# A decoder layer on one core: input tiles of the matmuls at two fixed offsets of SBUF, sample state multiplied in halves

## The chip, the cores and the metric

One Trainium2 chip, one of its cores. The metric is the time of one execution on the device in microseconds (us), as the median of the runs of a kernel.

## The reference

One step of a hybrid decoder layer in float32, for 256 prompt tokens and 8 sample tokens (264 columns in all), model width 2048:

```python
def decoder_layer(h, p, conv_buf, xbc_buf, h0, ...):
    h = h + 0.5 * rmsnorm(swiglu(rmsnorm(h, n1), w1_gate, w1_up, w1_down), n1_post)
    mix, cb, xb, hs = token_mixer(rmsnorm(h, n_mix), conv_buf, xbc_buf, h0, w_in, ..., w_out)
    h = h + rmsnorm(mix, n_mix_post)
    h = h + 0.5 * rmsnorm(swiglu(rmsnorm(h, n2), w2_gate, w2_up, w2_down), n2_post)
    gate = sigmoid(rmsnorm(h, n_ple) @ w_ple_gate)
    h = h + rmsnorm(gate * (p @ w_ple_proj), n_ple_post)
    return h, cb, xb, hs
```

The token mixer projects to 81 column tiles of 128, runs a gated convolution of width 31 on 1024 of the channels and a chunked state-space scan (48 heads, 8 groups, state 128) on the rest, and projects back. For each sample token it also reads the old state (`hst`), takes its product with that token's C vector, and writes the new state. The last three rows of the projection's xBC part are an output as well (`xo`).

## The kernel before

All activations lie feature-major: a tile is 128 features by 264 tokens. Every product with a weight matrix is made of three matmuls per 128 x 128 block (`mm3`, lines 242 to 246): weights and inputs are each split into a high half rounded to float32r and the low half that rounding left, and the sum takes high x high (L244), high weights x low input (L245) and low weights x high input (L246). For each of the three the weights are loaded anew and 264 columns of the input stream through.

**Inputs.** `split` (L248) makes an input tile out of a 128 x 264 tile: ScalarE writes the high half, VectorE the low half. `act_tile` (L193) takes the memory for both from a pool, `[P, 2, T]` float32, with 32 buffers of 2112 bytes per partition, the low half 1056 bytes behind the high one. In the built program buffer i begins at byte 89312 + 2112 i of each partition. Since 89312 is 348 x 256 + 224 and 2112 is 8 x 256 + 64, the high halves begin at 224, 32, 96 or 160 modulo 256 in turn, and the low halves 32 further, at 0, 64, 128 or 192. Each of the four kinds carries about a quarter of the matmuls.

**Weights.** They stream in units of up to 16 blocks (`Weights.load`, L135), each unit in halves of 8 blocks: one DMA of 512 KB on SyncE's queue (L150), the rounding on ScalarE (L151), the rest on VectorE (L152). Raw, high and low have four buffers each, and all of these begin at 224 modulo 256. The DMA queue of SyncE carries the weights and all other loads and stores in one order.

**Order.** FFN 1, the first part of the per-layer embedding, the mixer, FFN 2, the rest of the embedding. Most products go through `gemm_one` (L342): one output tile at a time, over 12 to 16 input tiles one after the other. `gemm_first` (L330) begins each product with four output tiles at once, so that one input tile serves four triples, 12 matmuls, in a row. In the mixer, the work of a state-space group (`ssd`, L678; `gate`, L769) is laid among the matmuls by a scheduler that runs when the program is built.

TensorE carries out its matmuls in the program's order, and the trace holds a record of every one of L244 to L246, 18,960 in all. So the n-th record is the n-th matmul of the program, and the input tile that a row of the trace read, and its address, are known from the built program.

**Sample state.** Lines 750 to 754: for each head pair j of a group, 1024 elements per partition of the old state are loaded (8 tokens x 128) into one of two buffers `h0`, GpSimd multiplies them by the C vectors, and VectorE sums each token's 128 products into `ych`.

**xBC rows.** `do_conv` (L598) copies the last 11 columns of each of 40 tiles to `xo`, one tile of 1760 bytes per partition, which L822 stores once at the end.

Of the kernel before, what the change touches and what calls it, by code (L numbers as in the profile page):

```python
# [9 lines left out]
F32 = mybir.dt.float32  # L10
F32R = mybir.dt.float32r
# [8 lines left out]
P = 128  # L20
NP_ = 256
NS = 8
T = NP_ + NS
DM = 2048
# [17 lines left out]
# ---------------------------------------------------------------- layout plan  # L42
def _in_order():
    """Column tiles of the input projection in the order they are computed."""
# [25 lines left out]
def _plan():  # L70
    """Weight units in order of use: (matrix, row tiles, column tiles), row tile slowest."""
# [39 lines left out]
# columns of the small-parameter block  # L111
# [13 lines left out]
class Weights:  # L125
    """Streams the weight units: load, round to float32r, keep what rounding left."""
# [8 lines left out]
    def load(self, between=()):  # L135
        """The next unit, in halves; runs a function of `between` ahead of each half."""
# [29 lines left out]
def kernel(ctx: ExitStack, tc: tile.TileContext, a: dict):  # L166
# [3 lines left out]
    cpool = ctx.enter_context(tc.tile_pool(name="cpool", bufs=1))  # L170
    wpool = ctx.enter_context(tc.tile_pool(name="wpool", bufs=4))
# [5 lines left out]
    # ------------------------------------------------------------ helpers  # L177
# [15 lines left out]
    def act_tile():  # L193
        return apool.tile([P, 2, T], F32R, tag="act", bufs=32, name=nm("act"))

# [32 lines left out]
    def table(name):  # L228
        """Functions that need a table run in program order, so that tables change only here."""
        if order["set"] != name:  # L230
            order["set"] = name
            after(nc.scalar.preload_act_table_set(name).ins)
# [15 lines left out]
    def split(x, gain=None):  # L248
        """float32r halves of x (times a gain per partition)."""
# [9 lines left out]
    class SumSq:  # L259
        """Sum of squares over tiles and partitions, on every partition. The last `direct` tiles  # L260
        go to the tensor engine by themselves."""
# [19 lines left out]
        def add_plain(self, s):  # L281
            """Adds the tile s itself."""
# [16 lines left out]
    def rsqrt(out, x, bias=0.0, scale=1.0):  # L299
        """(scale * x + bias) ** -0.5"""  # L300
        act(out, x, AF.Ln, bias=bias, scale=scale)
        act(out, out, AF.Exp, scale=-0.5)

    def rms_scale(p, n):
        """1 / sqrt(p / n + eps)"""
# [4 lines left out]
    # ------------------------------------------------------------ constants  # L310
# [10 lines left out]
    # ------------------------------------------------------------ residual stream  # L321
# [5 lines left out]
    bg = deque()  # work that fills in between the matrix products  # L327

    # ------------------------------------------------------------ feed-forward
# [22 lines left out]
    def ffn(xs, sq, done):  # L352
        """xs: split gained input; sq: its sum of squares. Calls done(m, y) on each finished
        column tile y (without the input scale); returns eps * (mean square + eps) of the input."""
# [42 lines left out]
    def ffn_scale(p, eq):  # L397
        """1 / 2 / sqrt(mean(y^2) + eps / scale^2): the post-norm of scale * y, halved, where
        eq = eps / scale^2."""
# [13 lines left out]
    # ============================================================ FFN 1  # L413
# [15 lines left out]
    # sample conv history: sums over the saved rows  # L429
# [33 lines left out]
    # y for the post-norm; h . y and y . y (with the gain) for the next pre-norm  # L463
# [22 lines left out]
    # mean square of h + rs y, from the parts  # L486
# [8 lines left out]
    # per-layer embedding projection: independent of the residual stream  # L495
# [13 lines left out]
    # u = rmsnorm(h + rs y), two tiles behind the update of h  # L509
# [15 lines left out]
    # ============================================================ mixer  # L525
# [3 lines left out]
    # causal triangle: row token s, column token l, l >= s  # L529
# [6 lines left out]
    tm = mp.tile([P, 2, 2, NH], F32, name="tm")          # token-major dt, dt*A per chunk  # L536
# [548 lines left out]
```

## Time and profile before

| | |
|---|---|
| median of 3 runs | 2482.04 us |
| lowest and highest | 2472.21 and 2486.53 us |
| span of the profiled execution, first to last instruction | 2479.2 us |
| its own time | not recorded apart from the span, which lies between the lowest and highest run, 2.8 us below the median |
| TensorE | 97% busy |
| VectorE, ScalarE, GpSimd | 64%, 48%, 14% busy |
| DMA | 490 MB, 198 GB/s |
| granted TensorE clock, mean | 0.990 |

A matmul's row in the trace has a start and a duration. The starts are measured; the ends are modelled, and successive matmuls overlap. What a matmul costs in a full stream is therefore the distance from its start to the next one's start, and for a stretch of a stream its length over the number of matmuls in it. The timeline prints starts to 0.01 us.

### The profile page before, as it was taken

The page shows a single profiled execution, that of the slowest core. Times are in us where ns is not written, and L with a number is a line of the kernel's source. Part 1 is how long each engine was busy: PE and PEld are TensorE (multiplying, and loading weights), DVE is VectorE, ACT ScalarE, POOL GpSimd, SP SyncE. Part 2 cuts the span into 40 slices and gives each one's busy share as a digit, 9 for nine tenths or more (in the row PEclk, how much of TensorE's full clock was granted, in tenths as well). Part 3 has the DMA queues.
Part 4 walks back from the last instruction along what each step waited for, and adds up shares of the span by engine and source line. Part 5 has one row for each costly group of instructions (what it writes and reads, how often), then busy time and mean ns, then how long its engine had stood idle before and what let it go on. Part 6 is the DMA issues. An engine that isn't in the chain of part 4 may idle for free.

```text
span 2479.2 us, 47214 instructions
## 1 busy us (share of the span) xinstructions
PE 2405.7 (97%) x19432; PEld 2380.9 (96%) x19432; DVE 1593.6 (64%) x2249; ACT 1179.2 (48%) x1761; POOL 348.6 (14%) x329
## 2 busy tenths in 40 slices
PE   8999999999999999999999999899999999999996
PEld 8999999999999889999998999899999999999996
DVE  6554455545557858979898965855545655555585
ACT  6444444433456465555655454544444443344463
POOL 2500000000015212121112011410000000000142
PEclk9999999999999999999999999999999999999998
DMA  7655555555556665666665547467666776675653
GB/s 242 211 181 180 180 179 179 180 180 181 181 167 214 200 199 191 214 208 197 210 212 187 180 162 231 140 232 235 221 211 221 237 236 206 210 239 191 193 171 114
DMA packets 160201, 489.88 MB, mean 198 GB/s; under 512 B 23360, under 2 KB 40304, under 8 KB 159984
## 3 DMA queue, kind: packets, MB, share of 16 engines
q1 hardware_dynamic: 159984, 486.85, 60.9%
q8 instruction: 152, 2.49, 0.4%
q14 instruction: 65, 0.53, 0.1%
HBM read 465.65 MB, written 22.42 MB: 197 GB/s over the span
## 4 chain that ended last, share of the span: by engine, by line
PE 86%; DVE 7%; DMA 2%; ACT 2%; issue 2%; POOL 1%; SPq 0%; DVEq 0%; ACTq 0%; POOLq 0%
PE acc L244 28%; PE acc L246 28%; PE acc L245 28%; DVE wlo L152 2%; DVE y L213 1%; DVE h L210 1%; DVE tmp L213 1%; ACT whi L151 1%; DVE act L213 1%; PE ps L729 1%; PE ps L296 0%; POOL run L210 0%; DMA ab<-d_cs 0%; PE ps L714 0%; DMA wraw<-in_w 0%
## 5 line engine op out<-in xcount | busy, mean ns | idle before, releaser
L244 PE MATMUL acc<-act,whi 128*128 128x264 f32 x6320 | 1801.0, 288 | 16.8 <-ACT whi L151 8.4
L245 PE MATMUL acc<-act,whi 128*128 128x264 f32 x6320 | 1804.2, 286 | 12.5 <-DVE act L213 6.3
L246 PE MATMUL acc<-act,wlo 128*128 128x264 f32 x6320 | 1802.4, 286 | 3.6 <-DVE wlo L152 3.6
L152 DVE TENSOR_TENSOR wlo<-wraw,whi 128x1024 fp32r<-128x1024 f32 (+1 forms) x806 | 992.3, 1233 | 612.7 <-ACT whi L151 610.0
L151 ACT CAST whi<-wraw 128x1024 fp32r<-128x1024 f32 (+1 forms) x806 | 828.1, 1031 | 994.7 <-PE acc L245 733.5
L245 PEld LDWEIGHTS acc<-act,whi 128*128 128x128 f32 x6320 | 1203.6, 190 | 17.9 <-DVE act L213 8.6
L246 PEld LDWEIGHTS acc<-act,wlo 128*128 128x128 f32 x6320 | 1199.1, 190 | 7.7 <-DVE wlo L152 5.2
L244 PEld LDWEIGHTS acc<-act,whi 128*128 128x128 f32 x6320 | 1186.6, 189 | 19.9 <-ACT whi L151 8.4
L210 POOL TENSOR_TENSOR run<-run,tmp 128x264 f32<-128x264 f32 x135 | 129.8, 962 | 982.3 <-ACT tmp L237 978.8
L210 POOL TENSOR_TENSOR s<-s,eap 128x1024 f32<-128x1024 f32 x24 | 47.3, 1972 | 608.2 <-DMA s<-in_hst 586.4
L213 DVE SCALAR_TENSOR_TENSOR y<-v,vec,y 128x247 f32<-128x247 f32 (+23 forms) x240 | 124.5, 540 | 1.1
L213 DVE SCALAR_TENSOR_TENSOR s<-bb,xds,s 128x128 f32<-128x128 f32 x192 | 52.6, 347 | 62.9 <-POOL s L210 62.9
L210 POOL TENSOR_TENSOR h<-h,cbc 128x1024 f32<-128x1024 f32 x24 | 65.4, 2738 | 165.3 <-DVE y L213 72.1
L210 DVE TENSOR_TENSOR tmp<-acc,rr 128x264 f32<-128x264 f32 x104 | 44.7, 431 | 64.0 <-PE acc L246 63.9
L252 ACT CAST act<-tmp 128x264 fp32r<-128x264 f32 x120 | 48.6, 409 | 62.3 <-DVE tmp L210 47.5
L210 DVE TENSOR_TENSOR tmp<-tmp,acc 128x264 f32<-128x264 f32 x88 | 37.6, 427 | 45.6 <-PE acc L246 44.8
L210 DVE TENSOR_TENSOR act<-tmp,act 128x264 fp32r<-128x264 f32 x120 | 54.3, 457 | 0.0
L210 DVE TENSOR_TENSOR y<-y,acc 128x264 f32<-128x264 f32 x80 | 34.0, 425 | 26.5 <-PE acc L246 26.5
L237 ACT ACTIVATE tmp<-tmp 128x264 f32<-128x264 f32 x112 | 46.8, 418 | 8.3 <-DVE tmp L210 8.0
L237 ACT ACTIVATE tmp<-y 128x264 f32<-128x264 f32 x67 | 28.1, 426 | 42.3 <-DVE y L210 41.2
L213 DVE SCALAR_TENSOR_TENSOR act<-h,vec,act 128x264 fp32r<-128x264 f32 x48 | 35.2, 756 | 6.4 <-ACT act L237 6.4
L237 ACT ACTIVATE act<-h,vec 128x264 fp32r<-128x264 f32 x48 | 23.8, 512 | 31.3 <-POOL h L210 15.2
(148 smaller groups left out, 800.7 us busy)
## 6 DMA issues: line engine op xcount, KB each, us to landing
wraw<-in_w SPq DMA_DIRECT2D x774, 512.0 KB, 4.7
h<-in_hst SPq DMA_DIRECT2D x24, 512.0 KB, 4.9
s<-in_hst SPq DMA_DIRECT2D x24, 512.0 KB, 6.4
out_nss<-s SPq DMA_DIRECT2D x24, 512.0 KB, 2.8
wraw<-in_w SPq DMA_DIRECT2D x32, 256.0 KB, 3.7
ab<-d_cs SPq DMA_DIRECT2D x16, 384.0 KB, 4.2
cbc<-d_bc SPq DMA_DIRECT2D x8, 512.0 KB, 4.2
bb<-d_bc SPq DMA_DIRECT2D x8, 512.0 KB, 7.4
```

The costliest lines, as they stand in the source:

```text
L151: nc.scalar.copy(hi, raw)
L152: nc.vector.tensor_tensor(out=lo, in0=raw, in1=hi.bitcast(F32), op=ALU.subtract)
L210: return (eng or nc.vector).tensor_tensor(out=out, in0=in0, in1=in1, op=op)
L213: return nc.vector.scalar_tensor_tensor(out=out, in0=in0, scalar=scalar, in1=in1, op0=op0, op1=op1)
L237: i = nc.scalar.activation(out=out, in_=in_, func=func, bias=bias, scale=scale)
L244: nc.tensor.matmul(acc, hi, x[:, 0, :], start=first, stop=False)
L245: nc.tensor.matmul(acc, hi, x[:, 1, :], start=False, stop=False)
L246: nc.tensor.matmul(acc, lo, x[:, 0, :], start=False, stop=last)
L252: nc.scalar.copy(t[:, 0, :], x)
L729: nc.tensor.matmul(pd[64 * q : 64 * q + 64, P * c : P * c + P], xdt[c][:, 2 * j + q, :], ab[c][:, 2 * j + q, :], start=True, stop=True,)
```

## The change

The input tiles get a pool of their own, `xpool`, allocated ahead of the weights. A buffer is 576 floats, 2304 bytes, which is 9 x 256, and of these the first 528 are used as before. The pool begins at byte 23264, which is 90 x 256 + 224. So every high half begins at 224 and every low half at 0 modulo 256; the weights stay at 224. The built program has these two offsets for all 18,960 matmuls.

The pool takes 6 KB more per partition. The tile `xo` becomes two rotating tiles of 10 pieces (2 x 440 bytes instead of 1760), each stored by three small DMAs once it is full. The state `h0` is loaded, multiplied and summed in halves of four tokens: 512 elements instead of 1024, three buffers of half the size instead of two.

```diff
+XSTRIDE = 576
...
+    xpool = ctx.enter_context(tc.tile_pool(name="xpool", bufs=32))
     wpool = ctx.enter_context(tc.tile_pool(name="wpool", bufs=4))
...
     def act_tile():
-        return apool.tile([P, 2, T], F32R, tag="act", bufs=32, name=nm("act"))
+        t = xpool.tile([P, XSTRIDE], F32R, tag="act", bufs=32, name=nm("act"))
+        return t[:, : 2 * T].rearrange("p (i t) -> p i t", i=2)
...
-    xo = mp.tile([P, 40, 3 + NS], F32, name="xo")
+    xos = {}
...
+    def xo_piece(i):
+        g = i // 3 if i < 24 else (i - 24) % 8
+        return g // 2, (i - 6 * (g // 2) if i < 24 else 6 + (i - 24) // 8 * 2 + g % 2)
+
+    def xo_runs(q):
+        return [((6 * q, 6), 0), ((24 + 2 * q, 2), 6), ((32 + 2 * q, 2), 8)]
...
     def do_conv(acc, i, out):
-        nc.scalar.copy(xo[:, i, :], acc[:, NP_ - 3 :])
+        q, e = xo_piece(i)
+        if q not in xos:
+            xos[q] = [mp.tile([P, 10, 3 + NS], F32, tag="xo", bufs=2, name=nm("xo")), 0]
+        nc.scalar.copy(xos[q][0][:, e, :], acc[:, NP_ - 3 :])
+        xos[q][1] += 1
+        if xos[q][1] == 10:
+            t = xos[q][0]
+            for (lo, n), src in xo_runs(q):
+                nc.sync.dma_start(a["xo"][:, lo : lo + n, :], t[:, src : src + n, :])
...
         for j in range(3):
-            h0 = mp.tile([P, NS, P], F32, tag="h0", bufs=2, name=nm("h0"))
-            nc.sync.dma_start(h0, a["hst"][3 * g + j])
-            tt(h0, h0, cbc, ALU.mult, nc.gpsimd)
-            nc.vector.tensor_reduce(out=ych[:, j, :], in_=h0, op=ALU.add, axis=AX.X)
+            for b in range(0, NS, 4):
+                h0 = mp.tile([P, 4, P], F32, tag="h0", bufs=3, name=nm("h0"))
+                nc.sync.dma_start(h0, a["hst"][3 * g + j][:, b : b + 4, :])
+                tt(h0, h0, cbc[:, b : b + 4, :], ALU.mult, nc.gpsimd)
+                nc.vector.tensor_reduce(out=ych[:, j, b : b + 4], in_=h0, op=ALU.add, axis=AX.X)
...
-                nc.sync.dma_start(a["xo"], xo)
```

Outside the mixer and the output projection behind it the order of the matmuls is the same row for row. In the mixer the scheduler places the parts of the state-space groups a little differently. On VectorE, in the first group's sample part, the sums of the state stood like this before (`wlo` is the low half of a weight buffer, `ych` the sums, `h` here the product with C):

```order
L152 TENSOR_TENSOR wlo_8_10350<-wraw_8_10348,whi_8_10349 128x1024
L152 TENSOR_TENSOR wlo_0_10405<-wraw_0_10403,whi_0_10404 128x1024
L754 TENSOR_REDUCE ych_9872<-h_496_9873 128x8
L152 TENSOR_TENSOR wlo_8_10411<-wraw_8_10409,whi_8_10410 128x1024
L754 TENSOR_REDUCE ych_9872<-h_497_9877 128x8
L152 TENSOR_TENSOR wlo_0_10479<-wraw_0_10477,whi_0_10478 128x1024
```

and stand like this now:

```order
L153 TENSOR_TENSOR wlo_8_10365<-wraw_8_10363,whi_8_10364 128x1024
L153 TENSOR_TENSOR wlo_0_10420<-wraw_0_10418,whi_0_10419 128x1024
L774 TENSOR_REDUCE ych_9875<-h_497_9876 128x4
L153 TENSOR_TENSOR wlo_8_10426<-wraw_8_10424,whi_8_10425 128x1024
L774 TENSOR_REDUCE ych_9875<-h_498_9880 128x4
L774 TENSOR_REDUCE ych_9875<-h_499_9884 128x4
L153 TENSOR_TENSOR wlo_0_10494<-wraw_0_10492,whi_0_10493 128x1024
```

Two sums of half the size stand where one stood, between the same pieces of weight work. On SyncE's queue, in the same group, the loads of the state (`h<-in_hst`) stood among the weight loads like this before:

```order
L150 DMA wraw_8_10483<-in_w 128x1024
L150 DMA wraw_0_10550<-in_w 128x1024
L752 DMA h_498_9881<-in_hst 128x1024
L150 DMA wraw_8_10556<-in_w 128x1024
L752 DMA h_555_10692<-in_hst 128x1024
L150 DMA wraw_0_10720<-in_w 128x1024
```

and now, with one of the new small stores of `xo` among them:

```order
L772 DMA h_502_9896<-in_hst 128x512
L151 DMA wraw_0_10750<-in_w 128x1024
L772 DMA h_559_10710<-in_hst 128x512
L151 DMA wraw_8_10756<-in_w 128x1024
L772 DMA h_560_10714<-in_hst 128x512
L772 DMA h_561_10718<-in_hst 128x512
L151 DMA wraw_0_10817<-in_w 128x1024
L619 DMA out_xo<-xo_9617 128x66
L151 DMA wraw_8_10823<-in_w 128x1024
```

A weight load now has one or two half loads ahead of it where it had one whole load; over the mixer there are 24 more state loads and 11 more stores of `xo` than before.

## Rows read from the trace of the kernel before

**Rows 1.** The page's busy times and the chain that ended last.

```profile
PE 2405.7 (97%) x19432; PEld 2380.9 (96%) x19432; DVE 1593.6 (64%) x2249; ACT 1179.2 (48%) x1761; POOL 348.6 (14%) x329
...
PE 86%; DVE 7%; DMA 2%; ACT 2%; issue 2%; POOL 1%; SPq 0%; DVEq 0%; ACTq 0%; POOLq 0%
```

**Rows 2.** Groups by form, the matmuls: busy us, mean ns; idle before, releasers.

```profile
L245 PE MATMUL acc<-act,whi 128*128 128x264 f32 x6320 | 1804.2, 286 | 12.5 <-DVE act L213 6.3 <-DVE act L210 6.0
L246 PE MATMUL acc<-act,wlo 128*128 128x264 f32 x6320 | 1802.4, 286 | 3.6 <-DVE wlo L152 3.6
L244 PE MATMUL acc<-act,whi 128*128 128x264 f32 x6320 | 1801.0, 288 | 16.8 <-ACT whi L151 8.4 <-ACT act L237 6.3 <-DVE h L213 1.4
```

**Rows 3.** Busy time by stretch: FFN 1, the mixer, FFN 2.

```profile
core 0: us, PE busy (x) PEld busy (x) DVE busy (x) ACT busy (x) POOL busy (x), PEclk, DMA share, GB/s
50.00:750.00 700.00, 700.00 (x5729) 700.00 (x5729) 357.31 (x396) 291.15 (x364) 44.67 (x80) 1.00 0.58 183
850.00:1400.00 550.00, 527.82 (x4237) 510.95 (x4236) 462.91 (x751) 313.59 (x568) 93.20 (x52) 0.99 0.63 199
1600.00:2340.00 740.00, 739.77 (x6050) 739.22 (x6049) 419.49 (x616) 307.63 (x382) 57.00 (x37) 1.00 0.67 219
```

**Rows 4.** Timeline of PE in FFN 1, first matmuls of five tiles: start, duration.

```profile
100.42 0.28 PE L244 MATMUL acc<-act,whi 128*128 128x264 f32 x1
...
100.78 0.29 PE L244 MATMUL acc<-act,whi 128*128 128x264 f32 x1
...
101.15 0.29 PE L244 MATMUL acc<-act,whi 128*128 128x264 f32 x1
...
101.52 0.29 PE L244 MATMUL acc<-act,whi 128*128 128x264 f32 x1
...
101.89 0.28 PE L244 MATMUL acc<-act,whi 128*128 128x264 f32 x1
```

**Rows 5.** Timeline of PE, output projection, first matmuls of five tiles used 12 times.

```profile
1394.97 0.28 PE L244 MATMUL acc<-act,whi 128*128 128x264 f32 x1
...
1396.42 0.29 PE L244 MATMUL acc<-act,whi 128*128 128x264 f32 x1
...
1397.91 0.29 PE L244 MATMUL acc<-act,whi 128*128 128x264 f32 x1
...
1399.37 0.28 PE L244 MATMUL acc<-act,whi 128*128 128x264 f32 x1
...
1400.82 0.28 PE L244 MATMUL acc<-act,whi 128*128 128x264 f32 x1
```

**Rows 6.** Timeline of PE in the mixer, first matmuls of three tiles.

```profile
926.54 0.28 PE L244 MATMUL acc<-act,whi 128*128 128x264 f32 x1
...
926.90 0.29 PE L244 MATMUL acc<-act,whi 128*128 128x264 f32 x1
...
927.27 0.28 PE L244 MATMUL acc<-act,whi 128*128 128x264 f32 x1
```

**Rows 7.** Groups by form: weight work on VectorE, the sample state's work.

```profile
L152 DVE TENSOR_TENSOR wlo<-wraw,whi 128x1024 fp32r<-128x1024 f32 x774 | 970.2, 1256 | 612.1 <-ACT whi L151 610.0 <-PE acc L246 0.8
...
L210 POOL TENSOR_TENSOR h<-h,cbc 128x1024 f32<-128x1024 f32 x24 | 65.4, 2738 | 165.3 <-DVE y L213 72.1 <-DMA cbc<-d_bc 30.6 <-DVE wlo L152 21.2
...
L754 DVE TENSOR_REDUCE ych<-h 128x8 f32<-128x1024 f32 x24 | 29.0, 1209 | 10.4 <-POOL h L210 10.3
...
L152 DVE TENSOR_TENSOR wlo<-wraw,whi 128x512 fp32r<-128x512 f32 x32 | 22.1, 690 | 0.6
```

**Rows 8.** Busy time by stretch, as in rows 3: two stretches with a crowded VectorE.

```profile
800.00:850.00 50.00, 43.43 (x320) 42.06 (x319) 46.71 (x72) 25.70 (x50) 18.65 (x19) 0.93 0.69 228
...
1350.00:1400.00 50.00, 47.17 (x371) 46.68 (x370) 49.86 (x93) 24.47 (x41) 6.04 (x6) 0.97 0.55 172
```

**Rows 9.** Waits of SyncE's queue: us in total, times, longest.

```profile
SPq L150 <- DVE wlo L152: 1342.6, 599, 13.1
...
SPq L752 <- DVE ych L754: 36.9, 20, 5.6
```

## Prediction

> **What bounds the kernel now.** I read the page's totals first, then the busy time by stretch, then single matmuls in the timeline. TensorE is busy 97% of the span and carries 86% of the chain that ended last [rows 1]. The stretches say more than the share: in FFN 1 and FFN 2 it is busy for 700.00 of 700 us and 739.77 of 740, while VectorE, the next busiest, has 357 and 419 [rows 3]. Nothing is waited for there, so those 1440 us are the number of matmuls times what one costs. That cost is 700 / 5729 = 122.2 ns and 740 / 6050 = 122.3 ns, at a granted clock of 1.00 [rows 3]. The mean of 286 to 288 ns of a row [rows 2] is not the price; rows overlap.
>
> The mixer is different: between 850 and 1400 us TensorE is idle for 22.2 of 550 us and VectorE is busy for 463 [rows 3].
>
> **Where the 122 ns come from.** In a timeline of FFN 1 I took the start of each tile's first matmul; the next such start is three matmuls later [rows 4]. The five tiles there begin at 224, 160, 96, 32 and again 224 modulo 256. The tile at 224 takes 100.78 - 100.42 = 0.36 us, 120.0 ns a matmul; the three others take 101.89 - 100.78 = 1.11 us, 123.3 ns a matmul. The pattern returns with every fourth tile. In the output projection one tile serves 12 matmuls in a row, so the printed hundredths weigh less [rows 5]: the tiles at 160, 96, 32 and 224 take 1.45, 1.49, 1.46 and 1.45 us, that is 120.8, 124.2, 121.7 and 120.8 ns a matmul. So a tile's offset goes with its price in both kinds of loop; 224 is the best or as good as the best in both, 96 among the worst.
>
> **The change, part by part.**
>
> *All high halves at 224, all low halves at 0.* 18,960 matmuls (three times 6320 [rows 2]) now pay 122.2 ns on average. Behind the change all are of the kind that now pays 120.0 [rows 4] to 120.8 ns [rows 5]. A stream in which every tile is of this kind and a new tile comes every three matmuls isn't in the trace, so these are the two ends. I take 120.2, nearer the first, because two thirds of the work runs in the loop of rows 4, and because the 12 matmuls of rows 5 contain the change-over from a slower tile. 2.0 ns x 18,960 = 37.9 us less; by the ends 41.7 and 26.5 us.
>
> *What of this the mixer keeps.* 4237 matmuls lie there [rows 3], so at most 8.5 us of the 37.9. Where TensorE waits for the end of a chain through ScalarE, VectorE and GpSimd, being earlier at the wait gains nothing. I take half as given back, 4.2 us; the ends are 0 and 8.5.
>
> *State in halves, VectorE.* 24 sums of 1209 ns become 48 of half the size. No half sum is in the trace. At least each costs half, which is nothing in all. The nearest pair is the weight work at 1024 and 512 elements, 1256 and 690 ns, a ratio of 0.55 [rows 7]; 48 x 0.55 x 1209 ns = 31.9 us against 29.0, so 2.9 us more. A third of it, 1 us, I put on the path, since VectorE is fully busy only in pieces of the mixer [rows 8]; the ends are 0 and 2.9. In the order the half sums stand between the same weight work, so nothing of a weight half is put behind more than one extra instruction.
>
> *State in halves, GpSimd.* 24 products of 2738 ns become 48: 65.4 us if each costs half, 131 if each costs as much as a whole one [rows 7]. GpSimd has 93 us of work in these 550 [rows 3], so even 66 more fit beside the rest; the sums now wait 10.3 us in all for these products [rows 7]. Nothing on the path. Should the cover go, the next in line is the gate of the following group.
>
> *Loads and stores on SyncE's queue.* 24 more state loads and 11 more stores of the xBC rows stand ahead of weight loads. The queue already waits 1.8 us each time for a state buffer (36.9 us in 20 cases), but 1342.6 us for a weight buffer [rows 9]: it is ahead of its consumers nearly always. The new waits are for three half buffers in place of two whole ones, so the queue can get less far ahead, by 512 elements per partition. Nothing on the path; if the cover fails it is the weight's rounding that comes late, at the price of some 2 us a time.
>
> *The moved mixer pieces.* The scheduler shifts parts of each group by some matmuls. The idle time that such places set is the 22.2 us of the mixer; I take no change, and a quarter, 6 us, in either direction for the ends.
>
> **The sum.** -37.9 + 4.2 + 1.0 = -32.7 us. Against the profiled span of 2479.2 us that is 2446.5. The span lies 2.8 us below the median of the runs, and I count from the median: 2482.0 - 32.7 = **2449.3 us**, 1.3% less. With all ends on the good side, -41.7 - 6 = -47.7, 2434; with all on the bad side (-26.5 + 1.4 ns x 4237 = 5.9 given back, + 2.9 + 6) -11.7, 2470. I don't expect all ends at once: 2436 to 2466.
>
> **The rivals.**
>
> *Nothing gained: the place is fast and not the offset.* In FFN 1 the tiles come in a fixed turn, so the cheap triple could be cheap because of what runs before it (a tile at 32) and not for its own offset. For this: in the mixer two tiles at 224 follow each other; the first takes 0.36 us and the second 0.37, as the slow kinds do [rows 6]. If every triple behind the change cost the 0.37 us of that second one, the matmuls would stay near 122 ns; only the mixer's items would be left and the time would be 2482 + 1 = 2483 us, with 6 to either side. Against it: in rows 5 a tile at 224 is followed by itself four times and still takes 1.45 us in all where the one at 96 takes 1.49. One page speaks for this rival: the Trainium skill, "SBUF — State Buffer", section "Specifications (TRN2)", has memory lines of 16 bytes as what a reading engine pays for. All eight offsets are multiples of 16, so by that rule no tile is dearer than another and the gain is nil; the 1.45 and 1.49 us of rows 5 speak against it as the whole story. I give this case 0.10.
>
> *Slower: VectorE ends last in the mixer.* Between 1350 and 1400 us VectorE is busy for 49.86 of 50 us, and TensorE loses 2.8; between 800 and 850, with VectorE at 46.71, TensorE loses 6.6 [rows 8]. More and smaller instructions on VectorE, and GpSimd beside them, could make each of the eight groups look like the latter. At 6.6 us a group that is 53 us, and 2449 + 53 = 2502 us. It decides from (32.7 + 12.4) / 8 = 5.6 us a group on, the point where the kernel is 0.5% slower. Against it: the mixer's TensorE now loses 22.2 us in all eight groups together, under 3 us a group, with VectorE at 84% [rows 3], and 2.9 us of new VectorE work are 0.4 us a group. 0.04.
>
> *The change doesn't do what it says.* The offsets depend on where the pool lands. In the built program they are 224 and 0 for all tiles, so this one has no share.
>
> **How the numbers follow.** 0.86 for the forecast, 0.10 for nothing gained, 0.04 for slower. The range from 2436 to 2466 holds the forecast with nearly all of its ends; left out are the two rivals and the outermost of the ends, under 2 in 10. About 0.5%, 12 us, is what a measurement of this kernel can tell from no change; its three runs lie 14 us apart. The forecast's whole range lies beyond that, nothing gained lies within, so the chances are 0.86, 0.10 and 0.04.
>
> **What would show it.** In FFN 1 the count of matmuls in 700 us should rise from 5729 to about 5824 (700 / 0.1202), with TensorE still busy throughout. The timeline there should show 0.36 us from one tile's first matmul to the next one's for every tile, with no pattern of four. In the mixer TensorE's idle time should be within 6 us of 22.2, VectorE's half sums near 665 ns. The prediction is wrong in its main step if the matmuls stay at 122 ns in FFN 1; it is wrong in its second if FFN 1 and FFN 2 are shorter by 1.6% and the mixer is longer.

## The result, and the profile after

| | before | after |
|---|---|---|
| median of 4 runs each | 2479.74 us | 2442.02 us |
| lowest and highest | 2472.21 and 2486.53 us | 2440.45 and 2448.86 us |
| span of the profiled execution | 2479.2 us | 2441.1 us |

The ratio is 0.9857, with a 95% interval from 0.9833 to 0.9881: 1.4% faster. The profiled execution of the changed kernel took 2442.84 us.

The page's busy times and chain of the changed kernel stand against [rows 1]:

```profile
PE 2365.9 (97%) x19432; PEld 2339.6 (96%) x19432; DVE 1584.4 (65%) x2273; ACT 1179.6 (48%) x1761; POOL 357.2 (15%) x353
...
PE 82%; DVE 7%; DMA 4%; issue 3%; ACT 3%; POOL 1%; SPq 0%; ACTq 0%; DVEq 0%; POOLq 0%
```

TensorE has the same 19,432 matmuls in 39.8 us less. VectorE has 24 instructions more and 9.2 us less, which the prediction had as about 3 us more; that is taken up below. The matmuls and the sample state by groups, against [rows 2, 7]:

```profile
L249 PE MATMUL acc<-act,wlo 128*128 128x264 f32 x6320 | 1796.9, 285 | 4.5 <-DVE wlo L153 4.4
L248 PE MATMUL acc<-act,whi 128*128 128x264 f32 x6320 | 1783.5, 283 | 14.6 <-DVE act L216 7.7
L247 PE MATMUL acc<-act,whi 128*128 128x264 f32 x6320 | 1766.0, 283 | 15.9 <-ACT whi L152 8.5
...
L213 POOL TENSOR_TENSOR h<-h,cbc 128x512 f32<-128x512 f32 x48 | 72.1, 1521 | 165.5 <-DMA cbc<-d_bc 77.8
...
L774 DVE TENSOR_REDUCE ych<-h 128x4 f32<-128x512 f32 x48 | 32.4, 677 | 16.3 <-POOL h L213 16.2
```

A half sum takes 677 ns and all 48 take 32.4 us, so 3.4 us more than the 24 whole ones. The stretches, with the columns of [rows 3]; the last is shorter than the one there, because FFN 2 now ends at 2320 us:

```profile
50.00:750.00 700.00, 700.00 (x5836) 700.00 (x5835) 366.63 (x408) 299.01 (x378) 50.32 (x89) 1.00 0.57 186
850.00:1400.00 550.00, 528.79 (x4310) 512.09 (x4309) 461.42 (x797) 317.03 (x572) 101.21 (x76) 0.99 0.64 202
1600.00:2300.00 700.00, 699.36 (x5823) 698.73 (x5822) 402.88 (x591) 292.07 (x358) 54.60 (x35) 1.00 0.67 222
```

FFN 1 holds 5836 matmuls in 700 us where it held 5729: 119.9 ns each by the window's count, and 120.0 ns by the distance between starts, at the same granted clock of 1.00. TensorE is idle for 21.2 us of the mixer's 550; this is the same stretch of time as in [rows 3], and not quite the same work, since the changed kernel is ahead by then. The timeline of FFN 1, every tile's first matmul, against [rows 4]:

```profile
100.03 0.28 PE L247 MATMUL acc<-act,whi 128*128 128x264 f32 x1
...
100.39 0.28 PE L247 MATMUL acc<-act,whi 128*128 128x264 f32 x1
...
100.75 0.28 PE L247 MATMUL acc<-act,whi 128*128 128x264 f32 x1
...
101.11 0.28 PE L247 MATMUL acc<-act,whi 128*128 128x264 f32 x1
```

Every tile takes 0.36 us, and the pattern of four is gone.

Where the 38.1 us of the two spans went, from the start of each stage's first matmul to the start of the next stage's first one. FFN 1 is counted from the start of the span, some 8 us ahead of its first matmul, and the last row to the span's end; each column is one execution. The table also holds two experiments told below: e2, the whole change but with the old spread of offsets, and e5, the old kernel with the state in halves.

| stage, us | before | e5 | e2 | after | after - before |
|---|---|---|---|---|---|
| FFN 1 | 788.3 | 787.8 | 787.8 | 774.3 | -14.0 |
| embedding, first part | 15.1 | 15.1 | 15.1 | 16.2 | +1.1 |
| mixer, input projection | 571.1 | 562.9 | 561.6 | 562.2 | -8.9 |
| mixer, output projection | 193.8 | 194.2 | 194.2 | 191.6 | -2.2 |
| FFN 2 | 788.8 | 788.0 | 788.0 | 776.1 | -12.7 |
| embedding, the rest | 122.2 | 121.9 | 122.0 | 120.7 | -1.5 |

### The profile page after: what moved, and what is told of

It is laid out like the page before. It is cut to its first block, busy times and chain, and to the rows that moved or that the text cites. A ratio compares the mean times of both kernels' runs of the same rounds, so it can differ in the third digit from the quotient of the medians.

```text
span 2441.1 us, 47358 instructions
## 1 busy us (share of the span) xinstructions
PE 2365.9 (97%) x19432; PEld 2339.6 (96%) x19432; DVE 1584.4 (65%) x2273; ACT 1179.6 (48%) x1761; POOL 357.2 (15%) x353
## 4 chain that ended last, share of the span: by engine, by line
PE 82%; DVE 7%; DMA 4%; issue 3%; ACT 3%; POOL 1%; SPq 0%; ACTq 0%; DVEq 0%; POOLq 0%
PE acc L248 27%; PE acc L247 27%; PE acc L249 27%; DVE wlo L153 2%; ACT whi L152 1%; DMA h<-in_hst 1%; POOL h L213 1%; DVE h L213 1%; DVE y L216 1%; DVE tmp L216 1%; DVE act L216 1%; DMA cbc<-d_bc 1%; DMA wraw<-in_w 1%; PE ps L299 1%; POOL run L213 0%
## 5 line engine op out<-in xcount | busy, mean ns | idle before, releaser
L248 PE MATMUL acc<-act,whi 128*128 128x264 f32 x6320 | 1783.5, 283 | 14.6 <-DVE act L216 7.7
L247 PE MATMUL acc<-act,whi 128*128 128x264 f32 x6320 | 1766.0, 283 | 15.9 <-ACT whi L152 8.5
L249 PEld LDWEIGHTS acc<-act,wlo 128*128 128x128 f32 x6320 | 1187.2, 188 | 8.5 <-DVE wlo L153 6.7
L216 DVE SCALAR_TENSOR_TENSOR y<-v,vec,y 128x251 f32<-128x251 f32 (+23 forms) x240 | 117.2, 508 | 1.2
L213 POOL TENSOR_TENSOR h<-h,cbc 128x512 f32<-128x512 f32 x48 | 72.1, 1521 | 165.5 <-DMA cbc<-d_bc 77.8
L774 DVE TENSOR_REDUCE ych<-h 128x4 f32<-128x512 f32 x48 | 32.4, 677 | 16.3 <-POOL h L213 16.2
```

The source lines that it names most:

```text
L213: return (eng or nc.vector).tensor_tensor(out=out, in0=in0, in1=in1, op=op)
L216: return nc.vector.scalar_tensor_tensor(out=out, in0=in0, scalar=scalar, in1=in1, op0=op0, op1=op1)
L247: nc.tensor.matmul(acc, hi, x[:, 0, :], start=first, stop=False)
L248: nc.tensor.matmul(acc, hi, x[:, 1, :], start=False, stop=False)
L249: nc.tensor.matmul(acc, lo, x[:, 0, :], start=False, stop=last)
L774: nc.vector.tensor_reduce(out=ych[:, j, b : b + 4], in_=h0, op=ALU.add, axis=AX.X)
```

## The experiments

e1 to e4, e5 to e8 and e9 to e12 each ran on one chip beside the kernel before, whose medians there were 2479.64, 2481.87 and 2481.30 us; ratios are to those.

### What a matmul's price hangs on

**e1_stream.** The layer is replaced by streams of 192 matmuls (64 triples), each with one offset of the weights and one of the input's high half, the low half 32 further as in the kernel before; then streams of other widths, and of halves at one offset.

```diff
...
+    for w in range(0, 256, 32):
+        for m in range(0, 256, 32):
+            stream(acc[i % 2], w, m, 64)
...
```

> The decoder layer is left out: zeros are stored, and TensorE runs streams of 64 triples (192 matmuls of 264 columns) on constant tiles, one stream for each pair of an input offset (high half, the low one 32 further) and a weight offset, modulo 256 bytes; then streams of other widths, and of high and low input at one and the same offset. Theory 'offset of the input': the price per matmul goes with the input offset alone, 120.0 ns at 224 for each of the eight weight offsets, about 121 at 160, 122 at 32, 123 to 124 at 96. Rival 'input against weights': what counts is the difference of the two offsets, so the table has equal prices along its diagonals, 120.0 where both are equal and 123 to 124 where they lie 128 apart. Rival 'no mixing': every stream of one fixed offset costs the same, 120 ns, since only changing offsets cost something.

The span is 2271.5 us and means nothing for the layer. Groups of the streams, PEld rows: `m96x,w224x` reads an input at 96 against weights at 224, the first number is the busy time of the 192. Over 192 it gives the price to 0.3 ns; the exact prices below are from the distance between starts.

```profile
L208 PEld LDWEIGHTS acc<-m96x,w224x 128*128 128x128 f32 x192 | 23.5, 188 | 0.0
L208 PEld LDWEIGHTS acc<-m128x,w0x 128*128 128x128 f32 x192 | 23.5, 188 | 0.0
L208 PEld LDWEIGHTS acc<-m224x,w96x 128*128 128x128 f32 x192 | 23.5, 188 | 0.0
...
L208 PEld LDWEIGHTS acc<-m96x,w96x 128*128 128x128 f32 x192 | 23.3, 188 | 0.0
L208 PEld LDWEIGHTS acc<-m224x,w224x 128*128 128x128 f32 x192 | 23.3, 188 | 0.0
...
L208 PEld LDWEIGHTS acc<-m192x,w0x 128*128 128x128 f32 x192 | 23.2, 188 | 0.0
L208 PEld LDWEIGHTS acc<-m32x,w96x 128*128 128x128 f32 x192 | 23.2, 188 | 0.0
L208 PEld LDWEIGHTS acc<-m160x,w224x 128*128 128x128 f32 x192 | 23.2, 188 | 0.0
...
L208 PEld LDWEIGHTS n264x<-m224x,w224x 128*128 128x128 f32 x192 | 23.1, 188 | 0.0
...
L208 PEld LDWEIGHTS n224x<-m224x,w224x 128*128 128x128 f32 x192 | 21.5, 192 | 0.0
...
L208 PEld LDWEIGHTS s96x<-m96x,w224x 128*128 128x128 f32 x192 | 23.7, 190 | 0.0
L208 PEld LDWEIGHTS s192x<-m192x,w224x 128*128 128x128 f32 x192 | 23.1, 187 | 0.0
```

The first three rows have neither the weights' offset nor the input's in common, only that the two are 128 apart; all three cost 122.2 ns. The next two are 0 apart, the three after them 192 (input less weights, modulo 256). Over all 64 pairs the price goes by that difference alone: 121.1 at 0 (in one stream 120.0), 121.3 at 32, 121.1 at 64, 121.7 at 96, 122.2 at 128, 160 and 224, 120.7 at 192. So the input's offset by itself is not the price. A second thing shows: the pair 224 and 224 cost 121.1 ns in one stream and 120.0 in another (`n264x`, 23.1 us). No stream of 264 columns went under 120.0. Down to 224 columns the price fell, to 111.7 ns; from there to 128 columns it stayed at 111.7.

The last two rows are of streams that read the low half from the high half's own place, not 32 further. At difference 128 (`s96x`) such a stream cost 123.3 ns where the one above cost 122.2, and at 224 (`s192x`) 120.0 where all eight with the low half 32 further cost 122.2. So the place of the low half counts as well, and the prices by difference hold for the layout of this kernel.

The prices of single streams also don't add up to the old mixture. Its four kinds of tile lie at differences 0, 192, 128 and 64, which alone cost 120.0 or 121.1, 120.7, 122.2 and 121.1 ns, 121.0 or 121.3 on average; mixed, they cost 122.2. By the starts in FFN 1 of the kernel before, the tiles at 224 and 96 cost 120.3 and 122.5 there, and those at 160 and 32 both 123.1, some 2 ns more than alone. So about half of the 2.2 ns between the old price and 120.0 goes with the change from one offset to another, and not with the four differences by themselves.

**e2_mixed_offsets.** The whole change, with the same order of instructions, but tiles 2112 bytes apart, so that the high halves begin at four offsets as before.

```diff
-XSTRIDE = 576
+XSTRIDE = 528
```

> The changed kernel with a stride of 528 floats instead of 576 in the new pool: four offsets in turn as in the kernel before, with everything else of the change kept (own pool, state in halves, small stores), and every engine's instructions in the same order as in the changed kernel. Theory 'offset of the input': 122.2 ns a matmul in FFN 1 again, about 5729 matmuls in 700 us, and a time of 2480 us with 6 to either side, so all of the gain is the offset's and the halves cost or give under 6 us. Rival 'own pool or smaller tiles': it stays near 2442 us.

2470.94 us (six runs, 2469.45 to 2472.54), ratio to before 0.9965, interval 0.995 to 0.998. FFN 1, the same stretch as above:

```profile
50.00:750.00 700.00, 700.00 (x5729) 700.00 (x5729) 357.48 (x397) 290.64 (x363) 45.31 (x80) 1.00 0.54 183
```

The count is back at 5729. By the medians the offsets are worth 2470.9 - 2442.0 = 28.9 us, and all the rest of the change 8.7 us, on the faster side. In the input projection this run and the changed kernel can be laid side by side, matmul by matmul, since their order is the same: the matmuls that follow each other within 140 ns in both take 5.8 us less in the changed kernel, and all the other distances are 6.4 us longer, so the projection is 0.6 us longer in all. Of the 6.4 us, 2.1 are matmuls at half the granted clock, of which the changed kernel's execution has 66 and this one 45 (more on these under e5); the rest is longer waits.

**e3_inputs_at_96.** All inputs at one offset still, but at 96 and 128, the place that [rows 5] had among the worst; weights at 224. Nothing is mixed any more.

```diff
+    xpool.tile([P, 32], F32, tag="pad", bufs=1, name="xpad")
...
+    wpool.tile([P, 32], F32, tag="pad", bufs=1, name="wpad")
```

> The changed kernel with 128 bytes of padding ahead of the input tiles and 128 ahead of the weights: every high input half at 96, every low one at 128, weights still at 224. Theory 'offset of the input': between 122.8 and 124.2 ns a matmul in FFN 1, that is 53 to 80 us more than the changed kernel, 2495 to 2522 us, slower than the kernel before. Rival 'no mixing': one fixed offset is enough, 120.0 ns and 2442 us. Rival 'input against weights': as the theory, the difference of the offsets is 128 here.

2472.43 us (2469.62 to 2478.68), ratio 0.9974, interval 0.9961 to 0.9987. FFN 1:

```profile
50.00:750.00 700.00, 700.00 (x5730) 700.00 (x5729) 357.80 (x397) 291.19 (x363) 45.01 (x80) 1.00 0.54 183
```

122.2 ns. That the tiles are all alike is not enough; it matters where they lie. At this place one price for all tiles happens to equal the mixture's. The price is that of e1 at difference 128, and below what the offset by itself would have given here.

**e4_weights_at_96.** The inputs stay at 224 and 0, and the weights move to 96.

```diff
+    wpool.tile([P, 32], F32, tag="pad", bufs=1, name="wpad")
```

> The changed kernel with 128 bytes of padding ahead of the weights alone: inputs at 224 and 0 as in the change, all weights at 96 instead of 224. Theory 'offset of the input': nothing changes, 120.0 ns a matmul in FFN 1, about 5836 matmuls in 700 us, 2442 us with 6 to either side. Rival 'input against weights': the difference is 128 as with inputs at 96, so 122.8 to 124.2 ns and 2495 to 2522 us.

2473.34 us, one run. FFN 1:

```profile
50.00:750.00 700.00, 700.00 (x5729) 700.00 (x5728) 357.75 (x397) 291.29 (x363) 43.85 (x80) 1.00 0.54 183
```

The inputs lie where the change puts them, and the gain is gone: 122.2 ns. This is the same difference of 128 as in e3, reached from the other side.

**e12_both_at_96.** Inputs at 96 and 128, weights at 96 as well: difference 0 at the place that was dear.

```diff
+    xpool.tile([P, 32], F32, tag="pad", bufs=1, name="xpad")
```

> The changed kernel with 128 bytes of padding ahead of inputs and weights both: inputs at 96 and 128, weights at 96. Theory 'input against weights' (the difference of the two counts): 120.0 ns a matmul in FFN 1, perhaps 121.1 where a stream begins the other way, and 2442 us with 6 to either side, although inputs at 96 alone and weights at 96 alone both gave 122.2 ns. Rival 'offset by itself': 122 ns or more, 2472 us.

2445.29 us (2443.37 to 2447.64), ratio 0.9866, interval 0.9849 to 0.9882. FFN 1:

```profile
50.00:750.00 700.00, 700.00 (x5836) 700.00 (x5835) 367.49 (x408) 299.12 (x378) 50.57 (x89) 1.00 0.57 186
```

The same 5836 as the changed kernel. With e3 and e4 this makes all four corners: (224, 224) and (96, 96) cost 120.0 ns, (96, 224) and (224, 96) cost 122.2.

**e8_stream_starts.** Streams of e1's kind, all with weights at 224, each started behind 48 matmuls of another width (64 to 256 columns). The layer is left out.

```diff
...
+    for c in (64, 128, 160, 200, 232, 256):
+        for m in range(0, 256, 32):
...
+            stream(warm, 32, 96, 16, c)
+            stream(out, 224, m, 64)
...
```

> As e1_stream, the layer left out, zeros stored: weights at 224, the eight input offsets, and ahead of each stream 48 matmuls of another width (64 to 256 columns), six widths. In e1_stream one and the same pairing, input and weights both at 224, ran at 121.13 ns in one place and at 120.00 in another. Theory 'remembered start': the price of a pairing is one of two or more steady values, set by how the stream begins, so that with difference 0 some of the six starts give 120.0 and others 121.1, and each keeps it for all 192 matmuls. Rival 'noise': all six starts give the same price within 0.1 ns. In either case a difference of 128 stays at 122.2 and is never under 122.

Groups of the streams, PEld rows; the number behind p is the width that ran ahead:

```profile
L208 PEld LDWEIGHTS p128x<-m64x,w224x 128*128 128x128 f32 x192 | 23.9, 188 | 0.0
...
L208 PEld LDWEIGHTS p128x<-m96x,w224x 128*128 128x128 f32 x192 | 23.5, 188 | 0.0
...
L208 PEld LDWEIGHTS p200x<-m96x,w224x 128*128 128x128 f32 x192 | 23.5, 188 | 0.0
...
L208 PEld LDWEIGHTS p200x<-m64x,w224x 128*128 128x128 f32 x192 | 23.4, 188 | 0.0
...
L208 PEld LDWEIGHTS p256x<-m224x,w224x 128*128 128x128 f32 x192 | 23.3, 188 | 0.0
...
L208 PEld LDWEIGHTS p128x<-m224x,w224x 128*128 128x128 f32 x192 | 23.1, 188 | 0.0
```

One and the same stream settles at one of two steady prices, and which one goes with what ran ahead of it: over the last 96 matmuls 120.0 or 121.1 ns at difference 0 (five starts and one), 121.7 or 124.5 at 96 (three and three), 120.7 or 120.0 at 192 (five and one). Behind 128 and more columns the first 48 cost up to 1.8 ns more than that, and seven of the eight streams behind 64 columns began at a granted clock of 0.50. Each start was run once. At 128 all six starts gave 122.2. The changed kernel's FFN 1 runs at the lower price of its pair.

### What the halves do

**e5_halves_alone, e6_xo_alone, e7_own_pool_alone.** The kernel before with one part of the change each: the state in halves (the part of the diff at L750 to L754); the rotating `xo` (the part at L543, L598 and L822); the inputs in a pool of their own with the old tiles of 2112 bytes.

```diff
+    xpool = ctx.enter_context(tc.tile_pool(name="xpool", bufs=32))
...
-        return apool.tile([P, 2, T], F32R, tag="act", bufs=32, name=nm("act"))
+        return xpool.tile([P, 2, T], F32R, tag="act", bufs=32, name=nm("act"))
```

> The kernel before with the state loaded, multiplied and summed in halves, and nothing else of the change: four offsets in turn, xo in one tile. In e2_mixed_offsets all of the change but the offsets gave 8.7 us, of which 9.5 us less in the input projection (561.6 us from its first matmul to that of the output projection, 571.1 in the kernel before). Theory 'halves': they are what gives it, 2471 us with 4 to either side and some 562 us in the projection. Rival 'xo' or 'pool': 2480 us and 571 us here.

> The kernel before with xo as two rotating tiles of ten pieces, stored in twelve small DMAs, and nothing else of the change. Theory 'halves': nothing here, 2480 us with 4 to either side, 571 us in the input projection. Rival 'xo': 2471 us and 562 us.

> The kernel before with the input tiles in a pool of their own ahead of the weights, at the old stride of 2112 bytes, so at the four old offsets, and nothing else of the change; the instructions stand in the old order. Theories 'halves' and 'xo': 2480 us with 4 to either side. Rival 'pool': 2471 us. Theory of the offsets: 122.2 ns a matmul in FFN 1 in any case.

| | median, us | ratio, interval | input projection, us |
|---|---|---|---|
| e5 | 2473.07 | 0.9960 (0.9946 to 0.9974) | 562.9 |
| e6 | 2476.35 | 0.9981 (0.9971 to 0.9992) | 569.9 |
| e7 | 2479.65 | 0.9988 (0.9977 to 1.0000) | 569.5 |

Against the 571.1 us of the kernel before, the halves alone take 8.2 us out of the input projection, which is nearly all that e2 has there. The two other parts stay within 0.2%. The interval of e6 leaves out 1, so `xo` gives a little by itself; and the execution of e6 that is shown took 2480.15 us, 3.8 above its median, so its 569.9 us are on the high side.

Part of the difference is TensorE's clock. In the kernel before, a wait of TensorE, and two stretches behind it with the columns of [rows 3]:

```profile
1067.95 0.71 PE L296 MATMUL ps<-run,ones 128*128 128x264 f32 x2 [1.83 <-POOL run L210]
```

```profile
1069.00:1072.00 3.00, 3.00 (x15) 3.00 (x15) 1.30 (x3) 2.96 (x6) 0.00 (x0) 0.50 0.75 253
1073.00:1075.00 2.00, 2.00 (x19) 2.00 (x18) 0.96 (x2) 2.00 (x5) 0.00 (x0) 1.00 0.06 23
```

TensorE had stood idle for 1.83 us. Behind that the granted clock was 0.50, the lower of the two levels (1.2 GHz), and matmuls started 0.22 us apart; then it was 1.00 (2.4 GHz) again and they started 0.12 us apart. In the input projection of the kernel before 87 matmuls start some 219 ns apart at the lower level, 8.5 us more than at the price of the others; in e5 there are 42, 4.1 us. So some 4.5 of the 8.2 us are clock, and most of the rest is shorter waits. The share differs from run to run: the runs of the kernel before have mean granted clocks from 0.989 to 0.993, and e7, with the old order of instructions, has 55 such matmuls. The stage times of one execution are therefore good to some 3 us, and the medians are the firmer ground.

How the halves shorten the waits is seen in one group. VectorE's timeline in the kernel before: a small sum, two of the pieces in which the convolution's y is summed, and the group's gate:

```profile
1336.32 2.38 DVE L210 TENSOR_TENSOR y<-y,vhist 128x8 f32<-128x8 f32 x1
1338.62 2.69 DVE L213 SCALAR_TENSOR_TENSOR y<-v,vec,y 128x255 f32<-128x255 f32 x1
...
1342.36 0.47 DVE L213 SCALAR_TENSOR_TENSOR y<-v,vec,y 128x254 f32<-128x254 f32 x1
...
1356.95 0.97 DVE L210 TENSOR_TENSOR h<-h,h 128x792 f32<-128x792 f32 x1
```

GpSimd's timeline beside it, the state's products:

```profile
1336.07 4.96 POOL L210 TENSOR_TENSOR h<-h,cbc 128x1024 f32<-128x1024 f32 x2 [14.31 <-DMA cbc<-d_bc]
1346.23 3.03 POOL L210 TENSOR_TENSOR h<-h,cbc 128x1024 f32<-128x1024 f32 x1 [5.21 <-DMA h<-in_hst]
```

While GpSimd multiplies two states, from 1336.07 to 1341.03, VectorE gets through two instructions, one of them on 8 columns, and they take 2.38 and 2.69 us, each about as long as a product (4.96 / 2); the next piece, with GpSimd at rest, takes 0.47 us. The third product waited 5.21 us for its state, whose load waits for one of the two buffers [rows 9]. The same group in e5, VectorE and then GpSimd:

```profile
1334.70 1.52 DVE L213 SCALAR_TENSOR_TENSOR y<-v,vec,y 128x252 f32<-128x252 f32 x1
...
1352.74 0.98 DVE L210 TENSOR_TENSOR h<-h,h 128x792 f32<-128x792 f32 x1
```

```profile
1333.95 4.67 POOL L210 TENSOR_TENSOR h<-h,cbc 128x512 f32<-128x512 f32 x3 [13.79 <-DMA cbc<-d_bc]
1340.37 1.30 POOL L210 TENSOR_TENSOR h<-h,cbc 128x512 f32<-128x512 f32 x1 [1.75 <-DMA h<-in_hst]
1342.71 3.48 POOL L210 TENSOR_TENSOR h<-h,cbc 128x512 f32<-128x512 f32 x2 [1.04 <-DMA h<-in_hst]
```

A blocked instruction takes 1.52 us now, the waits for a state are 1.75 and 1.04 us, and the gate comes 4.2 us earlier, of which 2.1 are there already when the first product starts. Over all groups GpSimd does not wait less for states: 22.7 us in 13 cases in e5, 16.4 in 5 before. The Trainium skill, "SBUF — State Buffer", section "🔬 SBUF: two separate sides", states a cause: a VectorE instruction with two inputs from SBUF and a GpSimd instruction that reads SBUF each take a shared pair of ports for the whole instruction, and the one that comes second stands still. The 2.38 and 2.69 us agree with it.

**e9_products_split, e10_three_whole_buffers.** They take the two things apart. e9 is the kernel before with only GpSimd's product cut in two (loads and sums stay whole); e10 leaves the product whole and gives the state three whole buffers, for which it needs the memory that e6 frees.

```diff
-            tt(h0, h0, cbc, ALU.mult, nc.gpsimd)
+            for b in range(0, NS, 4):
+                tt(h0[:, b : b + 4], h0[:, b : b + 4], cbc[:, b : b + 4], ALU.mult, nc.gpsimd)
```

```diff
-            h0 = mp.tile([P, NS, P], F32, tag="h0", bufs=2, name=nm("h0"))
+            h0 = mp.tile([P, NS, P], F32, tag="h0", bufs=3, name=nm("h0"))
```

> The kernel before with the state loaded and summed whole as it was, and only GpSimd's product made in two instructions of 512 elements. In the kernel before, VectorE's two-input pieces stand still for up to 2693 ns where a product of GpSimd runs, in the kernel with halves for up to 1522 ns. Theory 'blocked VectorE': the shorter product is what the halves gave, so the longest such piece is near 1.5 us and the time is 2473 us with 4 to either side (562 to 564 us in the input projection). Rival 'earlier loads': the smaller buffers are what helped, since a load waits only for a half to be summed; then nothing here, 2481 us and 571 us.

> The kernel of e6_xo_alone with three whole buffers for the state instead of two: loads can run ahead by one more, products and sums stay whole. Theory 'blocked VectorE': nothing, 2476 us with 4 to either side as in e6, longest blocked piece near 2.7 us. Rival 'earlier loads': 2469 us with 4 to either side, no load of the state waited for by GpSimd in the last group.

e9: 2474.32 us, ratio 0.9976 (0.9967 to 0.9985), input projection 566.4. e10: 2472.90 us, ratio 0.9973 (0.9961 to 0.9986), input projection 566.3. Instructions by tile, VectorE's pieces of y, min, median and max in ns; before, e9, e10:

```profile
L213 DVE SCALAR_TENSOR_TENSOR y<-v,vec,y x240: 437/464/2693, 947.1 to 1442.7; 128x253 f32<-128x253 f32 x8, 128x255 f32<-128x255 f32 x7, 128x251 f32<-128x251 f32 x7, 128x249 f32<-128x249 f32 x7
```

```profile
L213 DVE SCALAR_TENSOR_TENSOR y<-v,vec,y x240: 437/466/1605, 945.9 to 1438.2; 128x229 f32<-128x229 f32 x8, 128x249 f32<-128x249 f32 x7, 128x247 f32<-128x247 f32 x7, 128x245 f32<-128x245 f32 x7
```

```profile
L213 DVE SCALAR_TENSOR_TENSOR y<-v,vec,y x240: 434/461/2698, 940.7 to 1438.2; 128x255 f32<-128x255 f32 x7, 128x253 f32<-128x253 f32 x7, 128x251 f32<-128x251 f32 x7, 128x249 f32<-128x249 f32 x7
```

And the page's busy times of e9, against [rows 1]:

```profile
PE 2402.6 (97%) x19432; PEld 2379.0 (96%) x19432; DVE 1587.2 (64%) x2249; ACT 1180.0 (48%) x1761; POOL 364.6 (15%) x353
```

In e9 the longest piece is down to 1.6 us, and VectorE needs 6.4 us less for the same 2249 instructions, with the loads as before. Its median is 7.0 us under the kernel before, clear of noise, most of the 8.8 of e5: the shorter product does gain. In e10 the longest piece is still 2.7 us, but GpSimd waits for no state any more. Its median is 8.4 us under the kernel before, and that of e6, which it is built on, 5.5; the two intervals overlap, so what the earlier loads are worth is not shown. By single executions the input projections give 571.1 - 566.4 = 4.7 us for the product and 569.9 - 566.3 = 3.6 us for the loads. That these add up to the 8.2 of e5 within 0.1 us is no evidence, at some 3 us of difference from the clock alone. No run halves the loads and sums and leaves the product whole.

**e11_quarters.** The changed kernel with GpSimd's products in pieces of 256.

```diff
-                tt(h0, h0, cbc[:, b : b + 4, :], ALU.mult, nc.gpsimd)
+                for q in (0, 2):
+                    tt(h0[:, q : q + 2], h0[:, q : q + 2], cbc[:, b + q : b + q + 2], ALU.mult, nc.gpsimd)
```

> The changed kernel with each half's product made in two instructions of 256 elements; loads and sums stay in halves. Theory 'blocked VectorE': the longest blocked piece falls to about 0.9 us and some 2 us more go, 2440 us with 4 to either side; GpSimd has 48 more instructions, some 10 us more work beside the rest. Rival 'earlier loads': no change or slightly slower, 2442 to 2446 us.

2443.70 us (2438.36 to 2449.22), ratio 0.9856 (0.9835 to 0.9878): no better than the changed kernel. The longest piece of y is down to 1029 ns, and the input projection of the execution shown to 558.2 us, 4.0 less. But FFN 1, ahead of it and with the same instructions and offsets, took 781.3 us instead of 774.3:

```profile
50.00:750.00 700.00, 700.00 (x5782) 700.00 (x5781) 362.75 (x403) 294.66 (x371) 47.28 (x84) 1.00 0.56 184
```

700 / 5782 = 121.1 ns, steady from 100 to 750 us: it is the upper price of e8's pair at difference 0. FFN 2 of the same execution ran at the lower. So this run can't tell what the quarters are worth; the next to settle would be what sets the price at the start.

## Why the prediction was right, and where its steps failed

The forecast of 2449.3 us and the direction held; the time came out 7.3 us lower and inside the range. Of these, 2.3 us are the starting point: the forecast counts from 2482.04 us, the median of three runs, and with a fourth it is 2479.74. The gain was 37.7 us against 32.7. The steps fared less evenly.

**High halves at 224, low at 0: right in kind, and its reason too simple.** The prediction took 120.2 ns between 120.0 and 120.8; FFN 1 runs at 120.0. Outside the input projection the changed kernel is 29.2 us shorter, and there are 18,960 less 3888 matmuls (81 tiles of 16 blocks, three each), so 1.9 ns each. Luck has a part in it: the 120.0 ns were read off tiles at 224 in a mixture, and e8 and e11 show that tiles all at one place can run at 121.1. And the reading of [rows 4, 5], "224 is the best or as good as the best", made a property of the place out of what is a relation: e4 has the place and no gain, e12 the gain at a place that the prediction had among the worst. Those rows could not tell the two apart, since every weight buffer lies at 224; what they did not vary should have been said.

**What the mixer keeps: half was too much.** Against e2, 5.8 us of shorter matmuls met 6.4 us of longer waits and slow-clock matmuls. The input projection kept nothing of the offsets that could be told from one execution each, where the prediction let the mixer keep 4.2 us of 8.5; e12 with 563.5 us against 561.5 in e3 and 563.7 in e4 says the same. The prediction has no term for the granted clock, and 2.1 of the 6.4 us are such. One of the waits that grew is that for the group's gated sum (`run`): 8.7 us in e2, which has the same order, and 10.6 us in the changed kernel, where TensorE comes to it earlier; before it was 12.3 us.

```profile
PE ps L296 <- POOL run L210: 12.3, 7, 2.8
```

```profile
PE ps L299 <- POOL run L213: 10.6, 8, 2.5
```

(The first row is from the waits of PE in the kernel before, from 803 to 1375 us, the second from those in the changed one, from 790 to 1353 us: us in total, times, longest.)

**The state in halves: wrong in sign.** The prediction counted the half sums rightly (665 ns forecast, 677 measured) and put +1.0 us on the path. The halves alone were worth 8.2 us in the input projection and 8.8 us in all (2481.87 - 2473.07). The step that failed is the one that costs VectorE and GpSimd each by its own work and finds "nothing on the path": the product of 2738 ns in [rows 7] is not only work of GpSimd, it also stops VectorE, in the last group from 1336 to 1349 us, right ahead of the stretch where [rows 8] show VectorE full. The row to read was in the trace: a piece of y that takes 464 ns as a rule and 2693 at most. e9, with nothing but the shorter product, is 7.0 us faster. Whether the 36.9 us of waits for a state buffer [rows 9], which the prediction held for harmless, cost anything stays open (e10).

**SyncE's queue, the moved pieces.** Nothing was forecast for them, with 6 us either way. e6 and e7 lie 0.2 and 0.1% under the kernel before, which for e6 is 5.5 us by the medians and was not looked into, and TensorE's idle time in the mixer moved by 1.0 us, from 22.2 to 21.2.

**The sum.** Two errors met in the mixer: the offsets gave some 5 us less there than forecast, the halves 9 us more, so that the total is near the forecast partly by luck. Outside it the forecast was 2.0 ns x (18,960 - 4237) = 29.4 us less, and 29.2 were measured, over somewhat more matmuls (15,072). The 1.1 us that the first part of the embedding takes longer were in no step. They lie in two gaps between its matmuls, at sums over FFN 1's output, of 0.37 us each before and 0.96 and 0.67 us now; e12 has the same two: another gain ahead of a wait.

**The rivals.** "The place is fast and not the offset" falls: with all tiles alike at the wrong distance nothing is gained (e3), and at the right one there is no pattern. The Trainium skill, "SBUF — State Buffer", section "Specifications (TRN2)", which the prediction put beside it, has lines of 16 bytes, with a penalty for each crossing to a new line. It does not cover what was measured: 96 and 224 are both multiples of 16 and differ by 2.2 ns against weights at 224. Much of the rival's idea does hold: tiles at 160 and 32 cost some 2 ns more in the mixture than alone (e1), and a stream's past decides between two prices (e8, e11). "VectorE ends last in the mixer" falls as well: the mixer got 8.9 us shorter.

## What to carry to other kernels

Where one engine is busy throughout, look for patterns in the distance between starts of equal instructions, and ask of each address what it is relative to: here it was the distance of the input from the weights, which a change of either one can win or lose, and the change of that distance from tile to tile. A long instruction of GpSimd should be costed also by what it stops on VectorE; the sign is a maximum far above the median in a group of equal instructions. A gain ahead of a wait can be lost at the wait, as the mixer's 5.8 us were. And where stages of single executions are compared, look at the granted clock first.

## What had not been expected of the hardware

- A float32r matmul of 264 columns with its own weight load, in a steady stream, costs mostly 120.0 to 122.2 ns, by the distance between input and weights modulo 256 bytes, at a granted clock of 1.00 (high halves; the low ones lie 32 further, and with both in one place the prices by distance are others). Streams that change the distance from tile to tile cost more than the average of their kinds, 122.2 against 121.0 to 121.3 ns. Why the distance matters isn't shown; no run separates the reading of the weights from that of the input.
- A steady stream keeps one of two prices, 120.0 or 121.1 ns at distance 0, 121.7 or 124.5 at 96 and 120.7 or 120.0 at 192, for as long as it runs, up to a whole FFN (e11). What in its beginning decides was not found.
- From 128 to 224 columns a steady stream costs 111.7 ns, whatever its width; only the first 48 matmuls of a stream cost less, 110.5 ns at 128 columns (e8).
- While GpSimd multiplies two tiles in SBUF, a VectorE instruction with two inputs there can stand still for about the whole product: 2.69 us where 0.46 is usual, and 1.5 to 1.6 us with products of half the length.
